# The Up product of an encoder layer: when weight blocks are asked for, and where squares stand in ScalarE's order

## The chip, the cores and the metric

The kernel runs on one core of a Trainium2 chip. Its engines work side by side, each through its own list of instructions in order: TensorE multiplies matrices (PE in the profile, its weight loads PEld), VectorE (DVE) and ScalarE (ACT) work on tiles element by element, GpSimd (POOL) does the same more slowly, and SyncE (SP) only asks for DMA transfers. ScalarE and GpSimd ask for transfers too. The metric is the device time of one execution in microseconds (us); all times here are in us unless marked ns.

## The reference

One layer of an encoder for 1536 tokens (1024 and 512) of width 1024, in float32. The part that matters here is the second half of the layer:

```
hn = _rmsnorm(h, norm_mlp_g[l])
h = h + jnp.square(jax.nn.relu(hn @ w_mlp_up[l])) @ w_mlp_down[l]
...
return _rmsnorm(h, norm_final_g)
```

`w_mlp_up` is 1024 x 4096, `w_mlp_down` 4096 x 1024. Ahead of it stands a mixer of tokens with two kinds of attention, which ends in `h`.

## The kernel before, in words

**The stages.** The mixer takes the first 1156 us. Then comes `mlp()` (line 1600 on): Up, `hn @ w_mlp_up` with relu and square, in two halves of 768 tokens each, and Down, the product with `w_mlp_down`, from 1668 to the end.

**Up, one half.** The 4096 columns are worked through in 16 column blocks of 256 (`fb`, or just block 0 to 15), by `run_up` (L1984) and `up` (L1809). A block is one 2 x 2 step of a fast matrix product that needs seven products in place of eight: `prod` multiplies one of seven combinations of the weight block's quarters (`A`) with one of seven combinations of the activations (`B`, made once for a half). Each number is split into two float16 parts, high and low, so a product is 4 x 3 = 12 matmuls of 128 x 384. The products run in the order 0, 1, 2, 3, 4, 6, 5 on four PSUM banks: a gets product 0 and later 5, b product 1, c products 2 and 4, d products 3 and 6. (In the first block of the first half, product 5 runs second, on a bank of its own.) Between them ScalarE and VectorE take results out: `s1` is ScalarE's copy of bank a, `u2` VectorE's sum of b and `s1`, `s5` ScalarE's copy of bank c (L1865) with `u2` added by VectorE (L1866). Product 4 writes bank c anew, so it waits for the copy `s5`; product 6 adds into bank d, so it waits for VectorE's add that has read d (L1848).

`put` makes one quarter of the result: VectorE's add (L1848), ScalarE's relu (L1849) and square (L1850), and a store into `ud` in DRAM that ScalarE asks for (L1851). `total` adds two such quarters on VectorE (L1840, `cs`), and SP asks for that store.

**The weights of a block.** `up_dma` (L1750) asks SP for the two halves of a block's weights, 512 KB each. Blocks 2, 5, 8, 11 and 14 go into a spare half of B's tiles (named B in the trace), the others into the pool of raw tiles (`raw4`, six of them, which also holds `hn` rows, the rows `hl` and the gain of the late norms, and later the results `ar` that Down reads). `up_steps` (L1774) is the list of the seven steps that make the next block's combinations: sums and differences `S` on VectorE, and `cut16`, one high cut on ScalarE (L1648) and one low cut on VectorE (L1649) for each.

**The scale of a block.** Each weight block has a scale made of the sum of its squares. Blocks 0 to 2 have theirs from earlier. For blocks 3 to 15, `chunk_scale` (L1655) gives two squares of 128 x 1024 on ScalarE (L1653, `sq`) and a step `take`: four tiny matmuls on TensorE (`sc`, L145), then single columns on VectorE and GpSimd. This is done in the first half only, in blocks 1 to 13, each for the block two further on. In blocks 4 to 11 of the first half and in most of the second, squares of Down's weights (`sqwd`) come on top, one at product 1 in the first half, two at products 1 and 4 in the second.

**Late norms.** Four groups of 128 tokens get their second norm only during the first half of Up, in blocks 2, 4, 6 and 8 (`late_norm`, L2039): `sums`, a square over 128 x 1024 on ScalarE (`xnl`, L1624) with a power on GpSimd, and `rows`, a multiplication on VectorE and a store into `hnd` asked for by GpSimd. `hn_load` (L1732) reads rows of `hnd` for the second half; `pair_t` transposes them on TensorE (`pt`, L446) and makes the second half's B.

**The order of the work.** `run_up` makes a list `side` of seven lists of steps; after each product `up` calls the next one, so `side[n]` is what is written into the program behind the n-th product. The framework's planner then orders each engine's instructions: in general by the place in the program and by what it thinks is ready, but instructions under `keep_in_program_order` stay in the order written. Those are the products, in `run_up` also the requests on SP through `W_S` and `up_dma` (while `pinned[0]` is set), and the late norms. The squares of the weights and the cuts are not among them.

Before, in the first half, block 2 and block 3 are both asked for behind the last product but one of block 0 (`side[6]`), behind the store of the first `total`. In the second half block 2 is asked for ahead of block 0's steps and block 3 at the start of block 0. From then on block `fb` asks for block `fb + 3`.

Of the kernel before, what the change touches and what calls it, by code (L numbers as in the profile page):

```python
# [40 lines left out]
NFB = FF // FB  # L41
# [33 lines left out]
def encoder(ctx: ExitStack, tc: tile.TileContext, xs, outs, w):  # L75
# [73 lines left out]
    def up_raw(raw, fb, i):  # L149
        return nc.sync.dma_start(  # L150
            raw,
            w["w_mlp_up"][0][i * 512 : (i + 1) * 512, fb * FB : (fb + 1) * FB].rearrange("(k p) c -> p k c", p=P),
        )
# [140 lines left out]
    def rstd(ss, n, width, name, pin=False):  # L294
        m = sml.tile([P, 8], F32, tag="ms", name=f"ms_{name}")
        op = nc.vector.tensor_scalar(m[:, :n], ss, 1.0 / width, EPS, op0=ALU.mult, op1=ALU.add)
        if pin:
            tc.keep_in_program_order(op)
        r = sml.tile([P, 8], F32, tag="rs", name=f"rs_{name}")
        nc.gpsimd.tensor_tensor(r[:, :n], m[:, :n], mhalf[:, :n], op=ALU.pow)  # L300
        return r
# [1297 lines left out]
    def mlp():  # L1599
# [39 lines left out]
        def raw4(name):  # L1639
            return rw.tile([P, D], F32, tag="rw", name=name)  # L1640
# [14 lines left out]
        def chunk_scale(fb):  # L1655
            raw = raw_up[0, fb]
            n = 48 + 2 * (fb % 8)

            def take():
                pt = bank(f"sc{fb}")[:, 0:1]  # L1660
                all_rows(pt, ones, [col(n), col(n + 1)], True)
                take_weight_scale(pt, col(32 + fb), col(fb), col(16 + fb))
                nc.gpsimd.tensor_scalar(col(16 + fb), col(16 + fb), svs[:, 17:18], 1.0, op0=ALU.mult, op1=ALU.mult)

            sums = [
                lambda i=i: row_sums(raw[i].rearrange("p k c -> p (k c)"), n + i, f"{fb}_{i}") for i in range(2)
            ]
            return sums, take
# [4 lines left out]
        def as_rows(t):  # L1673
            return t.rearrange("p a k c -> p (a k c)")[:, 0 : 2 * D].bitcast(F32)
# [57 lines left out]
        def hn_load(b, j):  # L1732
            res = []
            for t in (j, j + 3):
                r0 = b * BT + t * P
                r = raw4(f"hn{b}_{t}")
                W_S.dma_start(r, hnd[r0 : r0 + P, :])
                res.append(r)
            return res


        raw_up = {}
        B1 = {}
        gl, hl = [], {}

        def late_load(r0):
            hl[r0] = raw4(f"hl{r0}")
            nc.gpsimd.dma_start(hl[r0], hd[r0 : r0 + P, :])

        def up_dma(st):  # L1750
            res = []
            for i in range(2):
                if st == (0, 0) and i == 1:

                    gl.append(raw4("gbl").rearrange("p (o c) -> p o c", o=1))
                    nc.gpsimd.dma_start(
                        gl[0],
                        bass.AP(
                            tensor=w["norm_mlp_g"].tensor, offset=w["norm_mlp_g"].offset, ap=[[0, P], [0, 1], [1, D]]
                        ),  # L1760
                    )
                    late_load(late_norms[0])
                if st[1] % 3 == 2:
                    r = as_rows((B0, B1)[st[0]]["spare", 4 + i])
                else:
                    r = raw4(f"rawu{st[0]}_{st[1]}_{i}")
                r = r.rearrange("p (k c) -> p k c", c=FB)
                op = up_raw(r, st[1], i)
                if pinned[0]:
                    tc.keep_in_program_order(op)  # L1770
                res.append(r)
            raw_up[st] = res

        def up_steps(st, ops):  # L1774

            nm = f"{st[0]}_{st[1]}"
            raw = raw_up.pop(st)
            a11, a21 = raw[0][:, :, 0:P], raw[0][:, :, P:FB]
            a12, a22 = raw[1][:, :, 0:P], raw[1][:, :, P:FB]
            S = {}  # L1780

            def one(i):
                if i == 0 and st == (0, 0):
                    ops[0] = (first_a0[0][:, 0], first_a0[0][:, 1])
                    return
                t = kh.tile([P, 2, 4, P], F16, tag="kh", name=f"A{nm}_{i}")
                if i in (1, 2, 3, 4) and not S:
                    for n in (0, 1, 2, 3):
                        S[n] = t2(f"S{n}_{nm}", (P, 4, P))
                if i == 1:  # L1790
                    nc.vector.tensor_tensor(S[0], a21, a22, op=ALU.add)
                    nc.vector.tensor_tensor(S[1], S[0], a11, op=ALU.subtract)
                if i == 3:
                    nc.vector.tensor_tensor(S[2], a11, a21, op=ALU.subtract)  # L1794
                if i == 4:
                    nc.vector.tensor_tensor(S[3], a12, S[1], op=ALU.subtract)
                src = {0: a11, 1: S.get(1), 2: S.get(0), 3: S.get(2), 4: S.get(3), 5: a12, 6: a22}[i]
                cut16(t[:, 0], t[:, 1], src, col(st[1]))
                ops[i] = (t[:, 0], t[:, 1])

            return [lambda i=i: one(i) for i in ((0, 5, 1, 2, 3, 4, 6) if st == (0, 0) else (0, 1, 2, 3, 4, 6, 5))]
# [104 lines left out]
        def raw_k4(name):  # L1906
            return k4.tile([P, D], F32, tag="k4", name=name)
# [66 lines left out]
        def spread(steps, n):  # L1974

            q, r = divmod(len(steps), n)
            res, at = [], 0
            for i in range(n):
                k = q + (i < r)
                res.append(steps[at : at + k])  # L1980
                at += k
            return res

        def run_up(b, A, B, last):  # L1984

            spare.update({n: B["spare", i] for n, i in enumerate((0, 1, 2, 3, 6))})
            for fb in range(NFB):
                An = {}
                new = None
                pinned[0] = True  # L1990
                if fb + 3 < NFB and (b, fb) != (0, 0):
                    up_dma((b, fb + 3))
                if 2 < fb + 2 < NFB and b == 0:
                    new = chunk_scale(fb + 2)
                side = up_steps((b, fb + 1), An) if fb + 1 < NFB else []
                more, at = last(fb)
                side = side + more
                if (b, fb) == (0, 0):
                    side = [[], []] + spread(side, 5)
                else:  # L2000
                    side = spread(side, 7)
                for n, steps in [*scales_of(b, fb).items(), *at.items()]:
                    side[n] += steps
                if new is not None:
                    for n, step in zip((0, 1), new[0]):
                        side[n].append(step)
                    side[5].insert(0, new[1])
                if (b, fb) == (0, 0):
                    side[6] += [lambda: up_dma((0, 2)), lambda: up_dma((0, 3))]
                up((b, fb), A, B, side)  # L2010
                A = An
                pinned[0] = False
# [26 lines left out]
        def late_norm(r0):  # L2039
            xn = raw_k4(f"xnl{r0}")  # L2040
            ss = sml.tile([P, 8], F32, tag="ss", name=f"ssl{r0}")
            r = []

            def sums():
                if r0 == late_norms[0]:
                    nc.gpsimd.tensor_scalar(
                        gl[0][:, 0, :], gl[0][:, 0, :], svs[:, 16:17], 1.0, op0=ALU.mult, op1=ALU.mult
                    )
                W_A.activation(xn, hl[r0], AF.Square, accum_out=ss[:, 0:1])
                r.append(rstd(ss[:, 0:1], 1, D, f"l{r0}", True))  # L2050

            def rows():
                W_V.scalar_tensor_tensor(
                    xn, hl.pop(r0), r[0][:, 0:1], gl[0][:, 0, :], op0=ALU.mult, op1=ALU.mult
                )
                nc.gpsimd.dma_start(hnd[r0 : r0 + P, :], xn)

            return {2: [sums], 4: [rows]}

        def last_0(fb):  # L2060

# [19 lines left out]

        A, B = {}, B1
        new_b(1, B)
        hn = {0: hn_load(1, 0)}
        for q in range(3):
            if q < 2:
                for g in range(2):
# [20 lines left out]
                    nc.gpsimd.dma_start(hd[r0 + j * P : r0 + (j + 1) * P, 512:1024], t, accum_op=ALU.add)  # L2108
        first_a = up_steps((1, 0), A)
        up_dma((1, 1))  # L2110
        up_dma((1, 2))
        for s in first_a:
            s()

# [114 lines left out]
        side = []  # L2229
        todo = []  # L2230
        scales = []
        for i, (p, g, j) in enumerate(order):
            si = i // NTB
            if j == 0:
                if si + 2 < len(stages):
                    b_dma(*stages[si + 2], raw_k4)
                side = spread(b_steps(*stages[si + 1]), 5) if si + 1 < len(stages) else []
# [31 lines left out]
            if g == NG - 1:  # L2269
                b, half = DEST[p][0]  # L2270
# [15 lines left out]
    for i, tr in enumerate(trunks):  # L2286
        run(tr, trunks[i + 1] if i + 1 < len(trunks) else None, i == 0)
    mix.close()
    mlp()


# [62 lines left out]
```

## Time and profile before

| | us |
|---|---|
| median of three runs | 2074.19 (2072.98 to 2076.94) |
| the profiled execution | 2076.11 |
| its span, first to last instruction | 2074.3 |
| TensorE busy in the span | 2025.4 |
| VectorE busy | 1529.8 |
| ScalarE busy | 1255.1 |
| Up, first half | 1156 to 1400 |
| between the halves | 1400 to 1439 |
| Up, second half | 1439 to 1668 |

A line of the timeline gives the start, the length, the engine, the source line, the operation with what it writes and reads, and the count; in brackets stands the time that the engine sat idle before it and whose end it waited for. Lines of the same kind that follow each other are merged into one. A list of waits gives the waiting engine and its tile, the releaser, and three numbers: total, times, longest. The rows by window give, for a stretch of time, how long each engine was busy in it, the clock that TensorE was granted (1.00 is full speed), the share of the DMA engines and what they moved.

### The profile page before, as it was taken

The numbers are of one execution on the slowest core, as the hardware profiler recorded it, in microseconds if no ns is written. First come the engines' busy times: TensorE is split into PE (matmuls) and PEld (weight loads), VectorE is DVE, ScalarE is ACT, GpSimd is POOL, SyncE is SP. The second block draws the span as 40 slices with busy tenths as digits, with TensorE's granted clock in tenths as the row PEclk, the third lists the DMA queues.
The fourth block names the chain that finished last, engine by engine and source line by source line (L and its number), as shares of the span: only waits on it lengthen the run. The fifth ranks groups of instructions, "written<-read, shape, count | busy, mean of one in ns | idle before, by whom it ended". The sixth has DMA issues, their size and how long they took to land. (4 is left out here: it accounts for less than half of the span.)

```text
span 2074.3 us, 31414 instructions
## 1 busy us (share of the span) xinstructions
PE 2025.4 (98%) x10589; PEld 1407.0 (68%) x10589; DVE 1529.8 (74%) x2909; ACT 1255.1 (61%) x2481; POOL 362.6 (17%) x505
## 2 busy tenths in 40 slices
PE   9999999999999999999999899999999999999998
PEld 8788878987797777777788565554666544444444
DVE  6775677778768865668863777788877778989653
ACT  5655664657646855667442588876888654544442
POOL 3233420321131212332102111113000000000000
PEclk9999999999999999999999999999999999999999
DMA  6436557645515646757774566559666599999442
GB/s 191 145 123 193 158 165 262 201 101 100 124 51 130 121 120 144 169 135 167 222 247 148 177 215 210 187 196 273 235 235 239 194 355 369 336 343 318 125 144 80
DMA packets 450347, 396.54 MB, mean 191 GB/s; under 512 B 168064, under 2 KB 383752, under 8 KB 450185
## 3 DMA queue, kind: packets, MB, share of 16 engines
q1 hardware_dynamic: 408247, 326.60, 53.0%
q10 hardware_dynamic: 36258, 50.88, 7.2%
q0 software_dynamic: 5680, 17.04, 3.0%
q8 instruction: 84, 1.38, 0.3%
q14 instruction: 78, 0.64, 0.1%
HBM read 283.21 MB, written 85.79 MB: 178 GB/s over the span
## 5 line engine op out<-in xcount | busy, mean ns | idle before, releaser
L316 PE MATMUL dn<-wd,a 128*128 128x512 f16 (+1 forms) x1872 | 403.4, 378 | 0.4 <-ACT a L1648 0.2
L316 PEld LDWEIGHTS <-A 128*128 128x128 f16 x2688 | 264.1, 99 | 197.3 <-issue 26.0
L316 PEld LDWEIGHTS <-a 128*128 128x128 f16 x2028 | 198.2, 98 | 237.2 <-DVE a L1649 1.1
L1648 ACT ACTIVATE a<-ar,gtab 128x512 f16<-128x512 f32 x168 | 115.3, 718 | 154.5 <-PE dn L316 60.5
L316 PE MATMUL gpss<-xs_0h,w_gs 128*128 128x512 f32 x512 | 182.1, 397 | 1.3 <-DVE ptls L992 1.3
L316 PE MATMUL uc<-B,A 128*128 128x384 f16 x768 | 137.9, 330 | 15.1 <-ACT s L1865 15.1
L1649 DVE SCALAR_TENSOR_TENSOR a<-ar,gtab,a 128x512 f16<-128x512 f32 x168 | 121.0, 749 | 37.4 <-ACT a L1648 36.7
L316 PE MATMUL ud<-B,A 128*128 128x384 f16 x768 | 136.7, 328 | 3.0 <-DVE c L1848 3.0
L316 PE MATMUL ua<-B,A 128*128 128x384 f16 x756 | 128.4, 326 | 0.8 <-DVE xrs L1558 0.8
L316 PE MATMUL ops<-wh_os,mgs 128*128 128x512 f32 x384 | 120.5, 391 | 0.0
L1649 DVE SCALAR_TENSOR_TENSOR A<-S,gtab,A 128x512 f16<-128x512 f32 x128 | 93.5, 748 | 36.1 <-ACT A L1648 35.9
L1648 ACT ACTIVATE A<-S,gtab 128x512 f16<-128x512 f32 x128 | 88.9, 716 | 42.3 <-DVE S L1794 24.2
L957 ACT ACTIVATE ps<-ss,nms 128x1024 f32<-128x1024 f32 (+1 forms) x96 | 93.4, 973 | 33.9 <-DVE ls L965 11.6
L316 PEld LDWEIGHTS gpss<-xs_0h,w_gs 128*128 128x128 f32 x512 | 96.0, 188 | 21.0 <-DVE ptls L992 1.5
L954 DVE TENSOR_REDUCE nms<-ss 128x1 f32<-128x1024 f32 (+1 forms) x96 | 99.6, 1039 | 13.4 <-PE ss L952 12.8
L316 PE MATMUL gpss<-xs_0l,w_gs 128*128 128x512 f32 x256 | 100.8, 394 | 0.0
L1210 POOL TENSOR_TENSOR bms<-rects,msks 128x384 f32<-128x384 f32 (+1 forms) x72 | 65.3, 917 | 153.1 <-DVE msbs L1226 111.0
L316 PE MATMUL gpss<-xs_1h,w_gs 128*128 128x512 f32 x256 | 91.6, 396 | 0.0
L1648 ACT ACTIVATE wd<-br,gtab 128x512 f16<-128x512 f32 x96 | 64.2, 715 | 29.7 <-PE dn L316 12.3
L316 PEld LDWEIGHTS ops<-wh_os,mgs 128*128 128x128 f32 x384 | 72.0, 188 | 14.7
L1230 ACT ACTIVATE pbs<-sbss,msbs 128x384 f32<-128x384 f32 (+1 forms) x96 | 55.4, 577 | 43.2 <-DVE msbs L1226 20.5
L977 POOL TENSOR_SCALAR pns<-ps,rcs 128x512 f32<-128x512 f32 x64 | 48.1, 751 | 176.5 <-DVE rcs L966 127.6
(367 smaller groups left out, 4781.7 us busy)
## 6 DMA issues: line engine op xcount, KB each, us to landing
ar<-ud SPq DMA_DIRECT2D x120, 512.0 KB
br<-in_w_mlp_down_dram SPq DMA_DIRECT2D x72, 512.0 KB
ud<-c ACTq DMA_DIRECT2D x128, 192.0 KB
rawu<-in_w_mlp_up_dram SPq DMA_DIRECT2D x44, 512.0 KB
raw_gs<-in_w_in_dram SPq DMA_DIRECT2D x32, 512.0 KB
B<-in_w_mlp_down_dram SPq DMA_DIRECT2D x32, 512.0 KB
zgs<-sgs ACTq DMA_DIRECT2D x48, 256.0 KB
ud<-cs SPq DMA_DIRECT2D x64, 192.0 KB
```

Of the source, the lines that this page charges most:

```text
L316: op = nc.tensor.matmul(out, a, b, start=start and n == 0, stop=stop and n == 2, **kw)
L954: nc.vector.tensor_reduce(nm_, s, axis=AX.X, op=ALU.max, negate=True)
L957: nc.scalar.activation(p, s, AF.Exp, bias=nm_, accum_out=l)
L977: nc.gpsimd.tensor_scalar(pn, p[:, 0 : NP * P], rlc, 1.0, op0=ALU.mult, op1=ALU.mult)
L1210: nc.gpsimd.tensor_tensor(bm.rearrange("p (r c) -> p r c", c=32), rects[h][:, ir : ir + kr_n, jr : jr + 32], msk[:, hf * 3 + ct, :].rearra ...
L1230: nc.scalar.activation(p[:, x], sb, AF.Exp, bias=nm_[:, x : x + 1], scale=-1.0, accum_out=l[:, x : x + 1])
L1648: nc.scalar.activation(hi, src, AF.Copy, scale=by)
L1649: nc.vector.scalar_tensor_tensor(lo, src, by, hi, op0=ALU.mult, op1=ALU.subtract)
```

## The change

Five things are moved, and nothing is added to or taken from the work.

- First half: block 2's weights are asked for behind the second product of block 0 (`side[1]`) and block 3's behind the fifth (`side[4]`), each at the head of its list.
- Second half: block 2's are asked for behind the fourth product of block 0 (`side[3]`) and block 3's behind the seventh (`side[6]`).
- The two squares of a weight block stand behind products 3 and 4 in block 1 (counted from 0) and behind 1 and 3 in blocks 2 to 13, in place of 0 and 1. The scale's step stands at 6 in block 1, and at 5 as before in the others.
- A late norm's square stands at 4 in place of 2, its multiplication and store at 6 in place of 4.
- The first two `hn` rows of the second half are asked for behind the first product of block 14 of the first half, in place of after the whole half.

```
-        B1 = {}
+        B1, hn = {}, {}
...
-                if fb + 3 < NFB and (b, fb) != (0, 0):
+                if 0 < fb < NFB - 3:
                     up_dma((b, fb + 3))
...
                 if new is not None:
-                    for n, step in zip((0, 1), new[0]):
+                    for n, step in zip((3, 4) if fb == 1 else (1, 3), new[0]):
                         side[n].append(step)
-                    side[5].insert(0, new[1])
-                if (b, fb) == (0, 0):
-                    side[6] += [lambda: up_dma((0, 2)), lambda: up_dma((0, 3))]
+                    side[6 if fb == 1 else 5].insert(0, new[1])
+                if fb == 0:
+                    for n, at_ in ((2, (1, 3)[b]), (3, (4, 6)[b])):
+                        side[at_].insert(0, lambda n=n: up_dma((b, n)))
+                if (b, fb) == (0, NFB - 2):
+                    side[0].append(lambda: hn.update({0: hn_load(1, 0)}))
...
-            return {2: [sums], 4: [rows]}
+            return {4: [sums], 6: [rows]}
...
-        hn = {0: hn_load(1, 0)}
...
         up_dma((1, 1))
-        up_dma((1, 2))
```

## Prediction

> **What bounds the kernel now.** I read the page's busy times first, then TensorE's waits in the Up part (1156 to 1668), then its timeline block by block, and last ScalarE's and SP's timelines ahead of each gap.
>
> ```profile
> PE 2025.4 (98%) x10589; PEld 1407.0 (68%) x10589; DVE 1529.8 (74%) x2909; ACT 1255.1 (61%) x2481; POOL 362.6 (17%) x505
> ...
> PE uc L316 <- ACT s L1865: 13.1, 11, 5.6
> PE ud L316 <- DVE c L1848: 1.4, 1, 1.4
> ...
> PE pt L446 <- DMA hn<-hnd: 1.9, 2, 1.3
> PE ud L316 <- DVE c L1848: 1.6, 3, 1.0
> ```
>
> TensorE is the bound: whatever closes a gap on it comes off the end, since the Down part behind Up has no appointment of its own. The second line (window 1140 to 1400: waiter, releaser, total, times, longest) is the first half of Up: eleven waits of product 4 for the copy `s5` that empties bank c. The last two lines are from 1400 on.
>
> ```profile
> 1156.08 2.12 PE L316 MATMUL ua<-B,A 128*128 128x384 f16 x12 [0.79 <-DVE xrs L1558]
> ...
> 1171.82 2.11 PE L316 MATMUL ua<-B,A 128*128 128x384 f16 x12
> 1173.77 2.11 PE L316 MATMUL ub<-B,A 128*128 128x384 f16 x12
> ...
> 1185.35 4.00 PE L316 MATMUL uc<-B,A 128*128 128x384 f16 x12 [5.57 <-ACT s L1865]
> 1189.14 2.71 PE L316 MATMUL ud<-B,A 128*128 128x384 f16 x12
> 1191.68 0.50 PE L145 MATMUL sc<-gtab 128*128 128x1 f32 x4
> ...
> 1205.69 0.50 PE L145 MATMUL sc<-gtab 128*128 128x1 f32 x4
> ...
> 1279.34 0.50 PE L145 MATMUL sc<-gtab 128*128 128x1 f32 x4
> 1291.61 2.94 PE L316 MATMUL uc<-B,A 128*128 128x384 f16 x12 [2.00 <-ACT s L1865]
> 1297.19 0.50 PE L145 MATMUL sc<-gtab 128*128 128x1 f32 x4
> ...
> 1340.94 0.50 PE L145 MATMUL sc<-gtab 128*128 128x1 f32 x4
> 1354.95 0.50 PE L145 MATMUL sc<-gtab 128*128 128x1 f32 x4
> ...
> 1438.78 2.11 PE L316 MATMUL ua<-B,A 128*128 128x384 f16 x12
> 1448.89 2.11 PE L316 MATMUL uc<-B,A 128*128 128x384 f16 x12 [1.95 <-ACT s L1865]
> 1453.91 4.06 PE L316 MATMUL ua<-B,A 128*128 128x384 f16 x24
> ```
>
> Columns are start, length, work, and in brackets the idle time before it with its releaser. A product is 1.95 (1171.82 to 1173.77), a block of seven 13.65; with the scale's four small matmuls a clean block is 14.01 (1191.68 to 1205.69, and again 1340.94 to 1354.95). From that I get what each stretch loses:
>
> - Block 0 of the first half: 1156.08 to 1171.82 is 15.74, 2.09 over 13.65.
> - Block 1: 1171.82 to 1191.68 is 19.86 where six products take 11.70: 8.16 lost.
> - Blocks 2 to 12: 1191.68 to 1354.95, eleven periods (twelve `sc` groups), is 163.27 against 11 x 14.01 = 154.11: 9.16 lost, of it 3.84 in block 8 (1279.34 to 1297.19 is 17.85).
> - Between the halves, 1.85 waiting for `hn` (the 1.9 above).
> - Block 0 of the second half: 1438.78 to 1453.91 is 15.13, six products 11.70: 3.43 lost.
>
> More is lost than the waits add up to, because the clock falls after them:
>
> ```profile
> core 0: us, PE busy (x), PEclk, DMA share, GB/s
> 1185.30:1187.30 2.00, 1.95 (x7) 0.50 0.01 3
> 1291.60:1294.40 2.80, 2.79 (x13) 0.70 0.00 0
> ```
>
> The granted clock is 0.50 behind the wait of 5.57, where two products (1185.35 to 1191.68) take 6.33 instead of 3.90, and 0.70 behind the wait of 2.00.
>
> **The change, part by part.** First, the requests for column blocks 2 and 3 of the first half.
>
> ```profile
> 1146.45 2.03 SPq L150 DMA_DIRECT2D rawu<-in_w_mlp_up_dram  x4
> 1173.33 0.34 SPq L1624 DMA_DIRECT2D ud<-cs  x1
> 1173.72 1.04 SPq L150 DMA_DIRECT2D B<-in_w_mlp_up_dram  x2
> 1174.81 3.03 SPq L150 DMA_DIRECT2D rawu<-in_w_mlp_up_dram  x4
> ...
> 1164.49 0.74 DVE L1649 SCALAR_TENSOR_TENSOR A<-rawu,gtab,A 128x512 f16<-128x512 f32 x1
> ...
> 1177.53 0.72 ACT L1648 ACTIVATE A<-B,gtab 128x512 f16<-128x512 f32 x1 [2.55 <-DMA B<-in_w_mlp_up_dram]
> 1181.04 1.06 ACT L1653 ACTIVATE sq<-rawu 128x1024 bf16<-128x1024 f32 x1 [2.78 <-DMA rawu<-in_w_mlp_up_dram]
> 1184.83 0.47 ACT L1865 ACTIVATE s<-uc 128x384 f32<-128x384 f32 x1
> ...
> 1455.90:1469.50 13.60, 13.60 (x85) 8.18 (x84) 11.08 (x20) 11.54 (x21) 0.00 (x0) 1.00 0.72 242
> ```
>
> SP asks in order. Both requests stand behind the store of a sum (`cs`, 1173.33), which waits for the sixth product, although SP has been free since 1148.5. Block 3 lands at 1181.04, and ScalarE, whose two squares of it stand at products 0 and 1, keeps `s5` behind them until 1184.83. The change puts four DMAs of 512 KB past that store. Block 2 goes into a spare half of B that nobody holds, so SP can ask for it right behind 1148.5. Block 3 needs the two tiles of block 0, whose last reader is the cut at 1164.49 (over at 1165.23): I expect its second half to be asked there. Block 2's rows took from 1173.72 to 1177.53, when ScalarE's cut starts on them; with 4 us block 3 is there by 1169.5, and its squares, now at products 3 and 4, come up some 10 us later. The store behind, at 1173.33, still finds SP free. So the wait of 5.57 goes and with it the slow clock. What is late next is the cut chain of block 2 on VectorE. Its analogue, block 1 of the second half, loses nothing: TensorE is busy 13.60 of the last row's 13.60. Of 8.16 I take 7.9; bounds 5.6 and 8.2.
>
> Second, ScalarE's order in blocks 2 to 13. Before, two squares stand at products 0 and 1, in blocks 4 to 11 a square of a Down weight at product 1, and in blocks 2, 4, 6, 8 the late norm's at product 2, all of them ahead of `s5`.
>
> ```profile
> 1290.04 1.05 ACT L1624 ACTIVATE xnl<-hl 128x1024 f32<-128x1024 f32 x1
> 1291.08 0.48 ACT L1865 ACTIVATE s<-uc 128x384 f32<-128x384 f32 x1
> ...
> 1249.30:1264.90 15.60, 14.13 (x89) 8.59 (x88) 11.43 (x21) 13.67 (x27) 2.42 (x4) 1.00 0.57 190
> ...
> 1469.50:1483.20 13.70, 13.70 (x87) 8.26 (x85) 11.12 (x20) 11.35 (x21) 0.00 (x0) 1.00 0.68 240
> ```
>
> A square holds ScalarE 1.04 (1290.04 to 1291.08). The change takes one square (now at 3) and the norm (now at 4) out of the way of `s5`: 2.08 in block 8, where the wait was 2.00, and 1.04 in the odd blocks. At most two squares then stand ahead of `s5`, as in block 12 before, which ran at 14.01. Nothing is removed: the same work comes behind `s5`. The last two rows (columns: us, TensorE, its weight loads, VectorE, ScalarE, GpSimd, clock, DMA) say whether it fits. Block 6, which carries every kind of square, keeps ScalarE busy 13.67, under 14.01; the second half runs a square at 1 and one at 4 with TensorE busy 13.70 of 13.70. Queued behind the moved work are `relu` and the high cuts; for these VectorE waits, and for its add on bank d the sixth product. That kind of wait cost 1.0 at most after 1400, and 1.4 once in block 0, where two blocks' cuts fall together. So the bounds are 0 and 1.0 for each of blocks 4 to 11; the others carry about the second half's load. I take 0.06, nearest to the second half's row, in all 0.5. The scale's matmuls stay behind product 5 (behind the last in block 1), a product or more after the squares. On GpSimd the norm's store changes places with the scale's steps, and the next `hl` load moves back some 4 us; its reader moves back as far. Gain 8.6 of 9.16.
>
> Third, `hn`.
>
> ```profile
> 1392.40 4.76 SPq L1624 DMA_DIRECT2D hn<-hnd  x2
> ...
> 1400.30:1438.80 38.50, 36.65 (x194) 19.47 (x194) 31.36 (x46) 26.22 (x47) 14.22 (x14) 1.00 1.04 321
> ...
> 1416.06 13.20 SPq L150 DMA_DIRECT2D rawu<-in_w_mlp_up_dram  x6
> 1429.25 0.73 ACT L1648 ACTIVATE A<-rawu,gtab 128x512 f16<-128x512 f32 x1 [6.39 <-DMA rawu<-in_w_mlp_up_dram]
> ```
>
> The two rows were asked at 1392.40; now in block 14, some 20 us sooner, ahead of block 15's `ar` and `br` requests. They hold two of six raw tiles; block 15's weights hold two, and the two `ar` of block 15 take the last. No request is pushed back by this. Gain 1.8 of 1.85, bounds 0 and 1.85.
>
> Fourth, block 0 of the second half. At the change of halves the DMA engines are full (share 1.04 at 321 GB/s). Its weights, asked at 1416.06, arrive at 1429.25 and hold ScalarE 6.39. The change takes 1 MB (block 2) out ahead of them, which at 321 GB/s is 3.3 us, and puts block 3's 1 MB behind; `hn`'s first 1 MB is gone from here too. Block 2 is now asked behind the Down loads, block 3 behind the first sum's store, still ahead of its use two blocks later. With the cut 3 us earlier the wait of 1.95 closes, but VectorE still works off two blocks' cuts as in the first half's block 0, which loses 2.09 without any of this. So I take a gain of 2.2, leaving 1.2; bounds 0 and 3.4.
>
> Block 0 of the first half: nothing in it moves on ScalarE or VectorE; 0 (at best 2.1).
>
> Sum: 7.9 + 8.6 + 1.8 + 2.2 = 20.5. The profiled execution took 2076.11 (span 2074.3 and 1.8 around it), so it would take 2055.6; the median of the runs, 2074.19, is 1.92 lower: 2053.7.
>
> **A rule against part of it.** Behind the wait of 2.00 the clock was 0.70 and block 8 lost 3.84, so I count 1.84 of it as the wait's consequence. The Trainium skill (TensorE: Matmul & The Clock Gate, Part 1: The HAM clock gate) says that the clock halves only after an idle window of about 3.4 us. By that rule a gap of 2.00 would not do it, and removing the gap would bring 18.7 in place of 20.5; the trace agrees for 5.57 and not for 2.00.
>
> **The rivals.** (1) The planner orders ScalarE by what it thinks is ready, and the squares are not fixed in program order: it might fill `s5`'s wait with them again. Against it: the second half's two squares stay apart well enough for 13.70 of 13.70. Then 9.16 stays, and the gain is 7.9 + 1.8 + 2.2 = 11.9: 2062.3. (2) Block 3's request sits on tiles that come free only with block 1's cuts, about 1174: the change does not do what it says there, 7.9 is lost, gain 12.6: 2061.6. Against it: the reader at 1164.49 is block 0's last. (3) The clock drop in block 8 has another cause than the gap and stays: 1.84 less, 2055.5. (4) Slower: the squares behind `s5` hold back `relu` and cuts, so VectorE's add on bank d comes late in the eight blocks 4 to 11, and each pays a wait of 2.00 with the clock's loss, 3.84 as block 8 did: 8 x 3.84 = 30.7, less 20.5, is 2084.4. It decides from 20.5 / 8 = 2.6 a block; ScalarE's 13.67 of 14.01 speaks against it.
>
> **How the numbers follow.** Forecast 0.68; (1) 0.12, (2) 0.07, (3) 0.06, (4) 0.05, and 0.02 for no change at all. The time is the forecast's, 2053.7. Its own bounds: all of 22.6 and block 0's 2.1 gained gives 2049.5; 1.0 lost in eight blocks gives 2061.7. Rivals (1) to (3) lie at or inside 2062.3, so 2049.5 to 2062 leaves out (4), half of (1) and a few oddities. A measurement here can tell 0.2% (4.1 us) from no change; every case but (4) and the last is beyond it. Being one reading of one trace, I shade it: faster 0.90, same 0.04, slower 0.06.
>
> **What would show it.** Right: `sc` groups 14.0 apart from block 2 to 12; no `uc` wait over 0.5 in the first half; clock 1.00 there; block 2's request on SP near 1149 and block 3's near 1165; no `pt` wait on `hn`; block 0 of the second half near 14.9. Wrong: waits of `ud` on VectorE's add in blocks 4 to 11, squares ahead of `s5` as before, ScalarE waiting for weights in block 1, or a new wait for `ar` or `br` near 1400.

## The result and the profile after

The changed kernel took 2060.49 us (2059.13 to 2062.72, four runs) and the kernel before 2074.06 beside it (2072.98 to 2076.94): ratio 0.9933, 95% interval 0.9916 to 0.9951. So 13.6 us are saved where 20.5 were forecast. The time lies inside the range and on the forecast's side, 6.8 us above the number.

The profiled execution of the changed kernel took 2062.72, with a span of 2060.8. From the page, the busy times, and from the list of waits in 1140 to 1400 the two rows that answer to the first two shown of before:

```profile
PE 2020.5 (98%) x10589; PEld 1406.1 (68%) x10589; DVE 1530.4 (74%) x2909; ACT 1252.9 (61%) x2481; POOL 363.1 (18%) x505
```

```profile
PE uc L316 <- ACT s L1865: 4.3, 5, 1.8
...
PE ud L316 <- DVE c L1848: 1.4, 1, 1.4
```

Eleven waits for `s5`, 13.1 us in all, became five with 4.3. Where they are left, TensorE's timeline shows:

```profile
1157.93 2.12 PE L316 MATMUL ua<-B,A 128*128 128x384 f16 x12 [0.79 <-DVE xrs L1558]
...
1174.09 2.11 PE L316 MATMUL ua<-B,A 128*128 128x384 f16 x12
...
1185.79 2.11 PE L316 MATMUL ua<-B,A 128*128 128x384 f16 x12
1187.73 0.50 PE L145 MATMUL sc<-gtab 128*128 128x1 f32 x4
...
1239.43 2.11 PE L316 MATMUL uc<-B,A 128*128 128x384 f16 x12 [1.35 <-ACT s L1865]
...
1356.28 0.50 PE L145 MATMUL sc<-gtab 128*128 128x1 f32 x4
...
1382.03 2.11 PE L316 MATMUL uc<-B,A 128*128 128x384 f16 x12 [1.82 <-ACT s L1865]
...
1387.88 1.91 PE L446 MATMUL pt<-ident,hn 128*128 128x128 f32 x16
...
1424.19 2.11 PE L316 MATMUL ua<-B,A 128*128 128x384 f16 x12
1426.84 0.50 PE L316 MATMUL ub<-B,A 128*128 128x384 f16 x2 [0.53 <-ACT A L1648]
1427.95 1.80 PE L316 MATMUL ub<-B,A 128*128 128x384 f16 x10 [0.61 <-DVE A L1649]
1435.58 2.11 PE L316 MATMUL uc<-B,A 128*128 128x384 f16 x12 [1.93 <-ACT s L1865]
1438.65 1.62 PE L316 MATMUL ud<-B,A 128*128 128x384 f16 x9 [0.96 <-DVE c L1848]
1440.60 4.06 PE L316 MATMUL ua<-B,A 128*128 128x384 f16 x24
```

Read as in the prediction: block 1's six products take 1174.09 to 1185.79, 11.70, exactly what they take without a wait. Block 5 has a wait of 1.35, block 15 one of 1.82, `pt` comes without a wait, and block 0 of the second half takes 16.41 (1424.19 to 1440.60), with two new waits in its second product. So, stage by stage, from the two profiled executions:

| stage | forecast | profiles |
|---|---|---|
| ahead of Up (nothing changed there; start 1156.08 and 1157.93) | 0 | -1.85 |
| first half, block 0 (15.74 and 16.16) | 0 | -0.4 |
| block 1 (8.16 lost, then 0) | 7.9 | +8.2 |
| blocks 2 to 12 (9.16 lost, then 2.24) | 8.6 | +6.9 |
| blocks 13 to 15 | 0 | -0.5 |
| change of halves, with both waits for `hn` | 1.8 | +2.3 |
| second half, block 0 (3.43 lost, then 4.71) | 2.2 | -1.3 |
| sum | 20.5 | 13.3 |

The new 2.24 of blocks 2 to 12 is the excess of the `sc` periods over 14.01: 1.50 in block 5, 0.37 in each of blocks 7 and 9, and none elsewhere.

SP's and ScalarE's timelines show the moved requests:

```profile
1150.37 2.19 SPq L150 DMA_DIRECT2D B<-in_w_mlp_up_dram  x2
1160.49 6.13 SPq L150 DMA_DIRECT2D rawu<-in_w_mlp_up_dram  x2
1175.59 0.34 SPq L1624 DMA_DIRECT2D ud<-cs  x1
...
1361.86 0.91 SPq L1624 DMA_DIRECT2D hn<-hnd  x2
...
1404.07 9.70 SPq L150 DMA_DIRECT2D rawu<-in_w_mlp_up_dram  x4
...
1181.06 0.47 ACT L1865 ACTIVATE s<-uc 128x384 f32<-128x384 f32 x1
1181.42 1.04 ACT L1653 ACTIVATE sq<-rawu 128x1024 bf16<-128x1024 f32 x1
...
1415.97 0.72 ACT L1648 ACTIVATE A<-rawu,gtab 128x512 f16<-128x512 f32 x1 [5.27 <-DMA rawu<-in_w_mlp_up_dram]
```

Block 2 is asked at 1150.37; block 3's second half is held until about 1166.6 (1160.49 + 6.13), when block 0's last cut has let the tile go, and the store of the sum behind it is not held up. In block 1 the squares stand behind `s5` (1181.42 behind 1181.06). But block 0 of the second half is still cut late: its weights are asked at 1404.07 and ScalarE starts on them 11.9 us later, having waited 5.27.

### The profile page after: what moved, and what is told of

It reads as the page before. It is cut to its first block, busy times and chain, and to the rows that moved or that the text cites. A ratio compares the mean times of both kernels' runs of the same rounds, so it can differ in the third digit from the quotient of the medians.

```text
span 2060.8 us, 31418 instructions
## 1 busy us (share of the span) xinstructions
PE 2020.5 (98%) x10589; PEld 1406.1 (68%) x10589; DVE 1530.4 (74%) x2909; ACT 1252.9 (61%) x2481; POOL 363.1 (18%) x505
## 4 chain that ended last, share of the span: by engine, by line
PE 41%; ACT 4%; DVE 3%; issue 1%; DMA 1%; ACTq 0%; POOL 0%; SPq 0%; POOLq 0%; DVEq 0%
PE dn L316 19%; PE ops L316 4%; PE ud L316 4%; PE ua L316 4%; PE uc L316 4%; PE ub L316 2%; PE ppbs L316 2%; PE dnf L316 1%; ACT A L1648 1%; DVE A L1649 1%; PE pt L446 1%; ACT sq L1653 0%; DMA br<-in_w_mlp_down_dram 0%; ACT c L1850 0%; DVE c L1848 0%
## 5 line engine op out<-in xcount | busy, mean ns | idle before, releaser
L1649 DVE SCALAR_TENSOR_TENSOR a<-ar,gtab,a 128x512 f16<-128x512 f32 x168 | 121.2, 749 | 38.6 <-ACT a L1648 37.7
L1649 DVE SCALAR_TENSOR_TENSOR A<-S,gtab,A 128x512 f16<-128x512 f32 x128 | 93.1, 748 | 25.7 <-ACT A L1648 25.4
L954 DVE TENSOR_REDUCE nms<-ss 128x1 f32<-128x1024 f32 (+1 forms) x96 | 99.7, 1039 | 14.0 <-PE ss L952 13.3
```

The source lines that it names most:

```text
L954: nc.vector.tensor_reduce(nm_, s, axis=AX.X, op=ALU.max, negate=True)
L1649: nc.vector.scalar_tensor_tensor(lo, src, by, hi, op0=ALU.mult, op1=ALU.subtract)
```

## The experiments

The first four ask which part brings what. The kernel before took 2072.81 us beside them (2070.83 to 2076.15).

**Requests alone.** The kernel before, with

```
-                    side[6] += [lambda: up_dma((0, 2)), lambda: up_dma((0, 3))]
+                    side[1].insert(0, lambda: up_dma((0, 2)))
+                    side[4].insert(0, lambda: up_dma((0, 3)))
```

> The kernel before with one part of the change: in the first half, block 2's weights asked behind the second product of block 0 and block 3's behind the fifth. Squares, late norms, hn rows and the second half as before. Theory (block 1's loss came from the late request alone): block 1, 19.86 from its first product to the scale's matmuls, falls by 7.9 to about 12.0; blocks 2 to 12 keep the 9.2 they lost, and the drop of the clock behind the wait of block 8 comes back; time 2074 - 8 = 2066. Rival (the squares at products 0 and 1 are at fault in block 1 too, since the scalar engine comes out of block 0 with work left over): 1.5 to 2 stay lost in block 1, time 2068. Second rival (the drop of the clock has nothing to do with the wait): a wait of about 2 in block 8 without a clock under 1.00 behind it.

Measured: 2066.07, ratio 0.9968 (0.9955 to 0.9981), 6.7 us less. From TensorE's timeline:

```profile
1179.34 2.11 PE L316 MATMUL uc<-B,A 128*128 128x384 f16 x12 [0.27 <-ACT s L1865]
...
1252.90 2.11 PE L316 MATMUL uc<-B,A 128*128 128x384 f16 x12 [1.45 <-ACT s L1865]
...
1282.94 2.11 PE L316 MATMUL uc<-B,A 128*128 128x384 f16 x12 [1.45 <-ACT s L1865]
```

Block 1's wait of 5.57 is 0.27, though the squares still stand ahead of `s5`; the block gains 7.7 of its 8.16. The other blocks keep their waits. But block 8 (the last row), with the old order untouched, waits 1.45 and loses 1.6 (its period is 15.63), not the 3.84 of the prediction's trace. What was different there stands on ScalarE's timeline of the kernel before:

```profile
1283.29 1.36 ACTq L1851 DMA_DIRECT2D ud<-c  x2
```

These two requests for stores take ScalarE 1.36 ahead of block 8's `s5`; in the run with the `hn` rows alone (below) the like two take 0.83, and that block waits 1.45 too. So 0.5 of the wait of 2.00 came from a slow request in that one execution, and the clock of 0.70 behind it made up the rest of the 2.2 us.

**Order alone.** The kernel before, with

```
-                    for n, step in zip((0, 1), new[0]):
+                    for n, step in zip((3, 4) if fb == 1 else (1, 3), new[0]):
...
-                    side[5].insert(0, new[1])
+                    side[6 if fb == 1 else 5].insert(0, new[1])
...
-            return {2: [sums], 4: [rows]}
+            return {4: [sums], 6: [rows]}
```

> The kernel before with the other part alone: squares at products 3 and 4 in block 1 and at 1 and 3 in blocks 2 to 13, late norms at 4 and 6; all requests and the hn rows as before. Theory (order and requests each bring what their place lost): blocks 2 to 12 lose 2.2 or less in place of 9.2; block 1 still loses most of its 8.2, because its first cut waits for block 2's rows until 21 after the start of Up; time 2074 - 7 = 2067. Rival (in block 1 it was the squares' place, not the request, that turned a late block into a lost one): block 1's wait for s5 shrinks from 5.6 to 1 or 2 and the clock stays up, time 2061, as much as the whole change.

Measured: 2067.14, ratio 0.9967 (0.9954 to 0.9979), 5.7 us less. Its profiled execution was 3 us shorter than its median: of the six executions two took 2063.07 and 2064.16 (the profiled one) and four 2066.93 to 2067.76. So its stages don't add up to the median; the waits are what it tells. TensorE's timeline and the clock behind the first wait:

```profile
1185.78 2.11 PE L316 MATMUL ud<-B,A 128*128 128x384 f16 x12 [2.90 <-DVE c L1848]
...
1240.76 2.11 PE L316 MATMUL uc<-B,A 128*128 128x384 f16 x12 [0.73 <-ACT s L1865]
1269.14 2.11 PE L316 MATMUL uc<-B,A 128*128 128x384 f16 x12 [0.20 <-ACT s L1865]
```

```profile
core 0: us, PE busy (x), PEclk, DMA share, GB/s
...
1186.80:1188.80 2.00, 2.00 (x14) 1.00 0.05 20
```

With the weights as late as before, block 1 loses 3.06 in place of 8.16: either part alone mends most of it, by another route. In the traces the parts therefore overlap there, 7.7 and 5.1 gained by each alone and 8.2 by both. The times don't show it: 6.7 and 5.7 add to 12.4, under the 13.6 of the whole change. So the theory's 2067 was met by luck: it let block 1 lose most of its 8.2, and in the trace it doesn't. What cost the four longer executions some 3 us isn't on record, nor whether the clock stayed up behind the gap of 2.90 in them. The wait in block 5 is here too, so it belongs to the new order.

**`hn` rows alone.** The kernel before, with the request for the first two rows in block 14.

```
+                if (b, fb) == (0, NFB - 2):
+                    side[0].append(lambda: hn.update({0: hn_load(1, 0)}))
...
-        hn = {0: hn_load(1, 0)}
```

> The kernel before with only the first two hn rows of the second half asked in block 14 of the first. Theory (the tensor engine gains between the halves what block 0 of the second half gives back, because that block's weights and cuts do not come sooner): the wait for hn, 1.85, goes, block 0 of the second half loses 1 to 1.5 more than its 3.4, and the time falls by under 1: 2073.3. Rival (nothing is given back): 2072.2.

Measured: 2073.08, ratio 1.0001 (0.9992 to 1.001). TensorE's timeline:

```profile
1433.10 2.11 PE L316 MATMUL ua<-B,A 128*128 128x384 f16 x12
...
1436.45 1.80 PE L316 MATMUL ub<-B,A 128*128 128x384 f16 x10 [0.61 <-DVE A L1649]
...
1444.08 2.11 PE L316 MATMUL uc<-B,A 128*128 128x384 f16 x12 [1.93 <-ACT s L1865]
1447.15 2.11 PE L316 MATMUL ud<-B,A 128*128 128x384 f16 x12 [0.96 <-DVE c L1848]
1449.10 3.09 PE L316 MATMUL ua<-B,A 128*128 128x384 f16 x18
```

Both waits for `hn` are gone, 1.85 us, and block 0 of the second half takes 16.00 (1433.10 to 1449.10) in place of 15.13: half of it is given back in that block, and the rest is below what the times can tell. In this run too block 8 lost 1.6 (period 15.62), and the old order's blocks 2 to 12 lost 6.82 in all, 7.15 in the run with the requests alone; the 9.16 of the prediction's trace held some 2.2 us that neither of these two executions has.

**The second half's requests.** The changed kernel with the requests for blocks 2 and 3 of the second half where they were.

```
-                for n, at_ in ((2, (1, 3)[b]), (3, (4, 6)[b])):
-                    side[at_].insert(0, lambda n=n: up_dma((b, n)))
...
         up_dma((1, 1))
+        up_dma((1, 2))
```

> The changed kernel with the second half's requests put back: block 2 ahead of block 0's steps, block 3 at the start of block 0. Theory (block 0's weights are held up by the raw tiles they wait for and by the accumulating stores beside them, not by the volume asked ahead of them): their first cut stays 8 to 9 ahead of the first product, block 0 of the second half still takes 16 to 17 to its second-last product, time within 1 of the changed kernel's 2060.5. Rival (the 1 MB taken out ahead of them counts at 321 GB/s): the cut comes 3.3 later, block 0 loses up to 3 more, time 2063.5.

Measured: 2060.49, ratio 0.9938 (0.9923 to 0.9953), and block 0 of the second half 16.17 against 16.41. This part of the change does nothing that the time or the block shows.

So what sets that block's 4.7 us? The next three take the changed kernel and turn to the weights' request, the order of the cuts, and the stores beside them. Beside these and the run behind them the kernel before took 2072.34 (2070.71 to 2077.63). The windows of the changed kernel show that the DMA engines were not full all along (columns: window, busy time of TensorE, its weight loads, VectorE, ScalarE and GpSimd, then clock, DMA share, GB/s):

```profile
1399.90:1403.90 4.00, 4.00 (x29) 2.73 (x28) 4.00 (x6) 4.00 (x8) 1.48 (x3) 1.00 0.06 17
1403.90:1407.90 4.00, 4.00 (x20) 1.85 (x19) 3.83 (x8) 3.08 (x7) 3.76 (x4) 1.00 0.99 260
1407.90:1411.90 4.00, 4.00 (x21) 1.79 (x19) 4.00 (x6) 2.79 (x5) 1.15 (x1) 1.00 1.08 218
```

For the 4 us up to 1403.9 they are all but idle, share 0.06: the request stands in SP's queue behind the third pair's `hn` rows, which by SP's list of waits are held up 7.0 us by VectorE's cut of `ar` rows (L1649). So the raw tiles are held by `ar` rows, not by `hn` rows as the next run's expectation says. From 1404 on they are full, with the third pair's rows, the weights and the first pair's accumulating stores on them; the second pair's stores come when the weights have landed. GpSimd's timeline of the changed kernel:

```profile
1402.82 3.65 POOL L2110 DMA_DIRECT2D hd<-dp  x4 [2.52 <-ACT dp L2108]
...
1417.56 3.55 POOL L2110 DMA_DIRECT2D hd<-dp  x4 [7.99 <-ACT dp L2108]
```

**Other tiles for block 0's weights.**

```
+                elif st == (1, 0):
+                    r = as_rows(B1["spare", i])
...
         new_b(1, B)
+        up_dma((1, 0))
...
-            else:
-                up_dma((1, 0))
```

> The changed kernel, with block 0 of the second half's weights landing in two other tiles that are free there, and asked straight after the first half's Up instead of behind the raw tiles that the hn rows hold; the cut steps stay where they stand in ScalarE's and VectorE's order. In the changed kernel block 0 of the second half takes 16.41 us against 11.70 of the same block-length without a wait, so 4.7 are lost in it. Theory (the late request, 1404.07, and the 11.9 us from it to the landing set the start of the block): the landing comes before pt, the loss of block 0 falls from 4.7 to 2-3 or the block starts 2-3 sooner, time 2057 to 2058.5, ratio to before 0.992. Rival (VectorE's and ScalarE's order sets it: the cut steps stand behind the Down work of the pair before them and cannot start sooner, whenever the weights land): no change, 2060.5, ratio 0.9938.

Measured: 2056.79, ratio 0.992 (0.9907 to 0.9932). SP's and TensorE's timelines:

```profile
1376.73 4.22 SPq L150 DMA_DIRECT2D B<-in_w_mlp_up_dram  x2
...
1421.20 2.11 PE L316 MATMUL ua<-B,A 128*128 128x384 f16 x12
1432.95 4.06 PE L316 MATMUL ua<-B,A 128*128 128x384 f16 x24
```

The block takes 11.75. All of its loss but 0.05 is gone, without a step of ScalarE or VectorE moved. That is more than I expected of it, and the rival, that the order of the two engines sets the block, falls.

**The cuts ahead as well.** The same, with block 0's cut steps ahead of the third pair's work.

```
+            if q == 2:
+                for s in up_steps((1, 0), A):
+                    s()
```

> As the run with the weights in the free tiles, and block 0's seven cut steps also written ahead of the third pair's Down work on ScalarE and VectorE. Theory that only the landing matters: the same as that run. Rival (the order of the two engines): here the block starts with its cuts done, the loss of block 0 falls from 4.7 to under 1, less what the third pair's work comes later for standing behind seven steps of 0.5 to 1 us (1 to 2 us): time about 2056.5 to 2058, ratio 0.992.

Measured: 2055.8, ratio 0.9916 (0.9902 to 0.9929); the block takes 11.74. Where nothing waits for weights, the order of the steps is worth nothing here.

**Without the accumulating stores** of the first two pairs. The kernel leaves out that part of the Down product.

```
-                for r0 in (0, BT):
+                for r0 in (0, BT) if q == 2 else ():
```

> The changed kernel without the accumulating stores of the first two pairs at the change of halves (part of the Down correction is left out of output columns 512 to 1023 in two thirds of those rows). Theory (the accumulating stores share the DMA engines with block 0's weights, which take 11.9 us from request to landing): the landing takes about 7 us, block 0 starts or ends 2 to 3 us sooner, time 2057.5 to 2058.5. Rival (request and raw tiles alone set it): landing 11 to 12 us, time 2060 to 2060.5.

Measured: 2055.81, ratio 0.9919 (0.9906 to 0.9933). SP's and ScalarE's timelines:

```profile
1401.12 9.70 SPq L150 DMA_DIRECT2D rawu<-in_w_mlp_up_dram  x4
...
1407.66 0.71 ACT L1648 ACTIVATE A<-rawu,gtab 128x512 f16<-128x512 f32 x1
```

Asked as late as in the changed kernel (15.9 us behind the first `pt`, there 16.2), the weights are there when ScalarE comes for them, 6.5 us later and not 11.9, and the block again takes 11.75. So the loss needs both, the late request and the stores beside it (the first pair's, 4 of 256 KB); taking either away removes it. How it reached TensorE stands on VectorE's timeline of the changed kernel:

```profile
1416.72 0.75 DVE L1649 SCALAR_TENSOR_TENSOR A<-rawu,gtab,A 128x512 f16<-128x512 f32 x1 [3.35 <-ACT A L1648]
```

VectorE, in order, waits 3.35 for ScalarE's cut and only then goes on with the third pair's rows and the block's other cuts. TensorE then waits in the second product for cuts, in the fifth for `s5` and in the sixth for VectorE's add, which all stand behind that work.

How tight this chain is shows in eight traces that ask for these weights late and keep the stores (before, changed, and six of the experiments). From ScalarE's first cut of the weights to the start of the second half's block 1 all have 24.62 to 24.67: 1429.25 to 1453.91 before, 1415.97 to 1440.60 in the changed kernel. Block 0 itself takes from 13.86 (order alone) to 16.41 in them. So the landing sets where the block ends, and a block that starts sooner only waits longer inside. The change brought the block's first product from 9.53 to 8.22 behind that cut, 1.31, and the block grew by 1.28.

**Block 15's side steps later.** In the changed kernel ScalarE's `s5` of block 15 (1381.50) stands behind four cuts of `ar` rows, the first of which wait for their DMA:

```profile
1378.67 1.33 ACT L1648 ACTIVATE a<-ar,gtab 128x512 f16<-128x512 f32 x2 [0.53 <-DMA ar<-ud]
```

Here they stand behind the third product.

```
+                elif (b, fb) == (0, NFB - 1):
+                    side = [[], [], []] + spread(side, 4)
```

> The changed kernel, with the side steps of the first half's block 15 (the rows asked of the accumulated result and the cuts on them) put behind its third product instead of its first, so that ScalarE's copies of banks c and d no longer stand behind steps that wait for a DMA. In the changed kernel that block waits 1.82 us for bank c. Theory: that wait goes, time 1.8 us less, 2058.7, ratio 0.993. Rival (the later steps hold up the change of halves by as much): the wait goes, and pt comes with a wait of the same size; time 2060.5.

Measured: 2058.3, ratio 0.993 (0.9916 to 0.9944). ScalarE's timeline:

```profile
1374.09 0.48 ACT L1865 ACTIVATE s<-uc 128x384 f32<-128x384 f32 x1
1374.46 2.55 ACT L1648 ACTIVATE a<-ar,gtab 128x512 f16<-128x512 f32 x4
```

`s5` is ahead of the cuts, the wait of 1.82 is gone, and no wait at `pt` takes its place: from the last `sc` to `pt` it is 29.80 us, in the changed kernel 31.60. Block 0 of the second half falls too, from 16.41 to 14.90 (1417.51 to 1432.41): the weights are cut 9.77 ahead of it, not 8.22. The ratio alone cannot tell this from the changed kernel.

**Both, and the late norms elsewhere.** Three kernels, beside which the kernel before took 2075.53 us: the weights in other tiles with block 15's steps later; the changed kernel with the norms in blocks 2, 6, 8, 10; and all of it.

```
-            n, odd = divmod(fb - 2, 2)
-            if 0 <= n < len(late_norms):
+            at_ = (2, 6, 8, 10)
+            odd = fb - 1 in at_
+            if fb in at_ or odd:
+                n = at_.index(fb - odd)
```

> The changed kernel with the two edits that gained by themselves: block 0 of the second half's weights in two free tiles and asked right after the first half's Up (2056.79 by itself), and the side steps of the first half's block 15 put behind its third product (2058.3 by itself). They lie at different places, so the gains should add: 1.8 and 4.3 us of stage time off 2060.5, so 2054.4, ratio 0.991 to 0.9915. Rival (the change of halves needs the rows that block 15's side steps cut, and with the weights no longer in the way these are the last): one of the two gains is lost, 2056.5 to 2057.

> The changed kernel with the late norms of blocks 4, 6, 8 put into blocks 6, 8, 10, so that block 4 has none. In every run with the new order of squares and norms so far block 5 waits 0.73 to 1.35 us for bank c, and one issue of a store of ScalarE's there takes 1.4 to 2.0 us where the like take 0.83. Theory A (the norm in block 4 pushes ScalarE into block 5): block 5's wait goes and the blocks after a norm lose the 0.37 us that blocks 7 and 9 lose; the time falls by about 1 us, 2059.5. Theory B (the slow issue is tied to a place in ScalarE's stream of instructions, not to the norm): with the norm's instructions gone from ahead of it, the slow issue of over 1.2 us stands some instructions later, in block 5 or 6; the wait there is 0 to 1.3 us; time 2059.5 to 2060.5. Seen in the issue rows and in the period of block 5, not in the total.

> Both edits of the run with the two gains, and the late norms in blocks 2, 6, 8, 10. Expected 2053.4 to 2054.4, ratio 0.9905 to 0.9915; theory A for block 5 says 1 us under the run with the two edits, theory B from nothing to 1.

Measured: 2054.16, ratio 0.9899 (0.9882 to 0.9915); 2059.37, ratio 0.992 (0.9905 to 0.9935); 2053.23, ratio 0.9894 (0.988 to 0.9909). The first has both gains in its trace, 29.84 from the last `sc` to `pt` and 11.77 for block 0. The last kernel has the lowest time: its interval lies wholly under the changed kernel's, 0.9916 to 0.9951, but not apart from the first of the three. For block 5, ScalarE's and SP's issues in the changed kernel:

```profile
1232.43 2.02 ACTq L1851 DMA_DIRECT2D ud<-c  x2
...
1232.57 1.98 SPq L1624 DMA_DIRECT2D B<-in_w_mlp_down_dram  x1
```

and in the kernel with the norms moved:

```profile
1230.45 0.83 ACTq L1851 DMA_DIRECT2D ud<-c  x2
...
1230.48 0.50 SPq L1624 DMA_DIRECT2D B<-in_w_mlp_down_dram  x1
```

In the changed kernel two queues at once take 2.0 us for issues that take 0.83 and 0.50 elsewhere; ScalarE stands still for 1.6, and block 5 loses 1.50. With no norm in block 4 both issues are short and block 5's period is 14.01. Theory B, a place in ScalarE's stream, falls in the form in which it was put: no store's issue of ScalarE's in the first half takes over 1.0 us there. Theory A holds for the rest: the 0.37 goes with the norm, for with norms in 6, 8 and 10 blocks 7, 9 and 11 have periods of 14.38, 14.52 and 14.37. Why the norm in block 4 goes with slow issues, and those in blocks 6 and 8 don't, stays open. That part is an association: all eight traces with the new order and a norm in block 4 have a slow issue on ScalarE there, 1.40 to 2.02, in three of them (order alone, block 15 later, the two together) with SP's at its usual 0.50. And the slow issue of 1.36 in block 8 of the kernel before shows that it can come elsewhere.

## Why the prediction was right, and where it was wrong

The mechanism of the first half held. **First, the requests:** block 2 asked at 1150.37 (forecast: right behind 1148.5), block 3 held until about 1166.6 (forecast: 1165.2), 8.2 gained where 7.9 were taken, and the run with this part alone ties it to the requests. What was not seen is that the order alone would have mended most of that block.

**Second, ScalarE's order:** the mechanism was right, and the size failed twice. The 9.16 to be won held some 2.2 us that one execution had: in two other runs with the old order block 8 lost 1.6, not 3.84, and half a microsecond of its wait was a slow request. I had written myself that the profiled execution stood 1.92 over the median, took that off, and counted the same excess as a gain as well. And of the 0.5 that I left behind `s5`, blocks 5, 7 and 9 kept 2.24, 1.50 of it in block 5, where the slow issues stand, and 0.37 in each block behind a moved norm: the work behind `s5` runs over into the next block's `s5`, where the sum had looked only at VectorE's add.

**Third, `hn`:** the gain came as forecast (2.3 with what follows from it, 1.8 taken), but the run with this part alone shows half of it given back in block 0 of the second half. I had looked for new waits on raw tiles and not asked what the earlier rows would meet: a block whose end the landing of its weights sets.

**Fourth, block 0 of the second half:** this step was wrong. It said that the change takes 1 MB out ahead of block 0's weights and that this is worth 3.3 us at full engines, 2.2 with what stays. In the code block 2's request stood behind blocks 0 and 1, not ahead; putting it back changes nothing (16.17 against 16.41). "The DMA engines are full" was a mean over 38.5 us; in the changed kernel's windows of 4 us they are all but idle just ahead of the request, until raw tiles come free, and full after it. The loss was set by a late request into stores that share the engines, and it grew by 1.3 in place of shrinking by 2.2.

So the 6.9 us missing from 20.5 are 3.5 from the fourth step, 2.2 from the one execution's excess and 1.7 from what stayed in blocks 5, 7 and 9, less 0.5 and 0.3 that `hn` and block 1 brought beyond their terms, plus 0.5 in block 15, whose wait for `s5` behind the `ar` rows went from 1.30 to 1.82. That is 7.1. The 0.2 more is less than the executions of one kernel differ by. The 2.3 us ahead of Up and in block 0 of the first half, where the change does nothing, are left out of this account as the difference of single executions: the profiled one of the changed kernel took 2.2 over its median.

Of the rivals, (1) did not happen: the squares stand where the change puts them. (2) did not: the tile came free with block 0's last cut. (4) did not: no `ud` wait on VectorE arose in blocks 4 to 11. (3) is half borne out. The drop did not stay: block 8 of the changed kernel has a period of 14.01. But that a gap of 2.00 alone makes the clock fall has the runs against it: in the one trace that has it a gap of 2.90 was followed by a clock of 1.00, gaps of 1.45 by products of 2.11, gaps of 5.57 and 5.78 by slow products. So the rule of the Trainium skill (TensorE: Matmul & The Clock Gate, Part 1: The HAM clock gate), by which an idle window of about 3.4 us is needed, agrees with these, and the clock of 0.70 behind the gap of 2.00 in the trace of before has a cause that no run here shows. It came late: 1.00 from 1291.60 to 1292.40, right behind the gap, and 0.50 from 1293.00 to 1296.00.

Of what the prediction listed as showing it wrong nothing came. Of what it listed as showing it right three things did not: `uc` waits over 0.5 stand in blocks 0, 5 and 15, the `sc` groups are 15.51, 14.38 and 14.38 apart in blocks 5, 7 and 9, and block 0 of the second half took 16.41, not near 14.9.

## What to carry to other kernels

Before counting a loss as a gain, look whether one execution's luck is in it: a block that loses 2 us more than its like is a suspect, above all where the profiled execution stands that much over the median. A DMA share averaged over 40 us says nothing on a request in it: cut the window to the few microseconds between request and landing, and look which tile the request waits for and what else then moves. The transfer that waited for a tile lent to something else was mended by another tile, not by the order of the work behind it. Before taking time out ahead of a block, ask what sets the block's end.

## What the runs showed of the hardware

Products after a gap of 2.90 us ran at the full clock, at 1.00 (in one trace), and those after 5.78 us took 4.00 for 12 matmuls in place of 2.11:

```profile
1184.30 4.00 PE L316 MATMUL uc<-B,A 128*128 128x384 f16 x12 [5.78 <-ACT s L1865]
```

(TensorE's timeline of the run with the `hn` rows alone.) Two issuing queues were slow at the same moment, 2.02 and 1.98 us for issues of 0.83 and 0.50 (cause open). And 1 MB of weights that lands within 6.5 us takes 11.9 beside 1 MB of accumulating stores.
